# Gated unit of the S5 branch as a job inside the recurrence's stage, and the modulation's gate row by products in four column groups

## The chip, the cores and the metric

One Trainium2 chip; the kernel runs on one of its cores. The metric is the device time of one execution in microseconds (us), median over runs.

## What is computed

One layer of a hybrid block over 1024 tokens (x, 1024 by 2048) with 256 context tokens: a modulation from a condition vector, a normalised and modulated input h, a wide projection h @ w_in (2048 by 6400), three branches (an S5 state space branch, a pooling branch, a two-directional RWKV recurrence), each times a SiLU gate, an output projection, and a last layer norm.

```
shift, scale, gate = split(silu(c) @ w_ada + b_ada, 3)
h = layernorm(x) * (1 + scale) + shift
s5_u, s5_g, pool_u, pool_g, rkv, rwkv_g, w_codes, a_codes = split(h @ w_in)

y_s5 = gelu(d_skip * u + state readout)              # 1024 x 512
y_s5 = y_s5 * sigmoid(y_s5 @ w_glu + b_glu)          # the gated unit, w_glu 512 x 512
y_pool, y_rwkv = ...
out = concat(y * silu(g)) @ w_out
x_new = layernorm(ALPHA * x + gate * out) * ln_g + ln_b
```

Two pieces matter here: the gated unit (the line with w_glu), and `gate`, the last third of the modulation, a row of 2048 numbers that w_out is multiplied with. All is computed in float32; the large products split each operand into a high and a low part and add three products.

## The kernel before, in words

The program has two large stages, written by two planners that fix each engine's order when the program is built.

**The projection's stage** (`phase_ab`, `adaln`, `in_proj`). All operations there are recorded by a helper, so they carry line L300 and are told apart by their tiles. TensorE multiplies one block of 128 features of w_in after another (`pm`, three products of 128x512 for each piece: `hi,whi`, `lo,whi`, `hi,wlo`); ScalarE makes `whi` and VectorE `wlo` for each piece, up to `AHEAD` = 3 pieces ahead. Beside it run side jobs, which a planner (`Sched`) puts between the products when their inputs should be ready by its own clock: the S5 blocks (`s5_run`, 16 blocks of two groups, on two lines that follow each other), then `s5_glu`; and, on another line (`others`), `ada_gate` followed by `pool_branch`. `misc`, a pair of PSUM banks, is shared by all of them. An S5 block ends with a GELU into tile `s5y`, which one DMA of ScalarE's queue stores to DRAM (`z_ys`).

- `ada_gate` computes the gate row. Each of 64 pieces of w_ada (`agraw`, 128x512) is multiplied by its 128 numbers of silu(c) and added to an accumulator on VectorE (`agacc`); after 16 pieces one product with a column of ones (`agone`) adds up the partitions. The row is stored as `z_mgate`.
- `s5_glu` is last on the S5 line. It loads w_glu and, in 32 DMAs, all of S5's output (`gluy`), and then, for each of four blocks of 128 features, makes 8 products of 128x512 in float32 (k = 0 to 3, two halves of the tokens), a sigmoid (`glus`), and on VectorE the products with the S5 output and with the SiLU gate (`glug`); a DMA stores the result in `z_y`.

**The recurrence's stage** (`phase_c`). Key tiles (`kq`, 512 KB each, 80 segments in all) are loaded by SyncE into a ring of `KEPT` = 13 tiles. For each segment TensorE makes a Gram matrix (`gp`), which VectorE masks (`aq`). Eight segments form a batch; a batch goes through DRAM (`flat`) into a triangular solve on VectorE (`solve`, lines L1880 and L1882: 62 operations in sequence, `tmp` and `nn`), and back. A `prefix` per pair of heads (`ping`) and then the recurrence itself follow: 8 pairs, each 16 steps that TensorE, ScalarE and VectorE pass on to each other (`banky`, `banku`, lines L2023 to L2067). In the gaps a planner (`Pace`) puts other jobs by rank, lowest first: jobs of the segments (0), `prefixes` (0.5), `solver` (1), finishing work (1.5), segment loads and Gram matrices (2), and the early part of the output projection (`out_first`, ranks 2.5 to 5: `ofacc`, the first 12 of 16 blocks of w_out's rows). Within an engine's queue, SyncE's too, the order so written is fixed: an instruction that waits holds up everything behind it.

The last part (`phase_d`) does the remaining output projection and the final norm.

## Time and profile before

| | |
|---|---|
| median of 3 runs | 2965.87 us (2957.72 to 2967.88) |
| the profiled execution's own time | 2957.1 us |
| its span, first to last instruction | 2955.3 us |
| TensorE busy | 2653.7 us (90%) |
| VectorE busy | 1985.1 us (67%) |
| ScalarE, GpSimd busy | 1032.9 us, 1149.9 us |
| mean granted TensorE clock | 0.947 of full speed |

The profile is one execution with every instruction's start and duration. Busy time is a sum over stages that have different limits, so what an engine's share means is read stage by stage. The profiled execution lies 8.8 us under the median of the runs.

### The profile page before, as it was taken

To read this page: it belongs to the slowest core of one execution; us is meant where nothing else is said; L and a number is where in the kernel's file an instruction comes from. 1 tells how busy PE (TensorE), PEld (TensorE's weight loads), DVE (VectorE), ACT (ScalarE), POOL (GpSimd) and SP (SyncE) were. 2 spreads that over 40 slices of the span, in tenths; PEclk is the share of its full clock that TensorE was granted. 3 is DMA by queue.
4 is the path that set the end of the run, shared out by engine and by line. 5 is a ranking of instruction groups with operands and counts; after the bars stand their busy time and mean duration, and the time that the engine had idled before them with its cause. 6 is when DMAs were issued, how large, how long until landed. Compare 5 with 4: busy or idle time off the path is not lost. (4 is left out here: it accounts for less than half of the span.)

```text
span 2955.3 us, 56419 instructions
## 1 busy us (share of the span) xinstructions
PE 2653.7 (90%) x20080; PEld 2156.8 (73%) x20080; DVE 1985.1 (67%) x4247; ACT 1032.9 (35%) x2611; POOL 1149.9 (39%) x1681
## 2 busy tenths in 40 slices
PE   7989999999999999999899777988888899789775
PEld 2258878888888887778778366877777778678664
DVE  5548235566666567888889375677876886686568
ACT  1321224444444443222222132444443444333222
POOL 0104003343333334223552033555655556456515
PEclk9999999999999999999999877999999999798898
DMA  8734646666666665656443466665665666646744
GB/s 282 259 114 139 153 120 176 159 168 191 180 172 170 171 182 144 169 158 169 117 122 110 148 225 158 182 181 154 185 187 161 177 165 178 157 126 188 239 152 159
DMA packets 698674, 498.49 MB, mean 169 GB/s; under 512 B 347182, under 2 KB 624406, under 8 KB 695574
## 3 DMA queue, kind: packets, MB, share of 16 engines
q1 hardware_dynamic: 672632, 449.52, 54.5%
q0 software_dynamic: 6912, 24.12, 2.9%
q10 hardware_dynamic: 18848, 21.24, 2.0%
q8 instruction: 159, 2.61, 0.4%
q14 instruction: 123, 1.01, 0.1%
HBM read 339.64 MB, written 155.07 MB: 167 GB/s over the span
## 5 line engine op out<-in xcount | busy, mean ns | idle before, releaser
L300 PE MATMUL pm<-hi,whi 128*128 128x512 f32 x1600 | 511.4, 401 | 4.2 <-ACT whi L300 4.2
L300 PE MATMUL pm<-hi,wlo 128*128 128x512 f32 x1600 | 509.4, 400 | 4.3 <-DVE wlo L300 4.2
L300 PE MATMUL pm<-lo,whi 128*128 128x512 f32 x1600 | 509.2, 400 | 0.0
L300 DVE TENSOR_TENSOR wlo<-wraw,whi 128x256 fp32r<-128x256 f32 x400 | 229.2, 579 | 318.8 <-ACT whi L300 308.9
L300 PEld LDWEIGHTS pm<-hi,whi 128*128 128x128 f32 x1600 | 275.0, 190 | 58.0 <-ACT whi L300 5.8
L300 PEld LDWEIGHTS pm<-hi,wlo 128*128 128x128 f32 x1600 | 275.2, 190 | 56.1 <-DVE wlo L300 6.3
L300 PEld LDWEIGHTS pm<-lo,whi 128*128 128x128 f32 x1600 | 274.3, 189 | 51.2 <-issue 2.2
L300 ACT ACTIVATE whi<-wraw 128x256 fp32r<-128x256 f32 x400 | 160.7, 414 | 413.4 <-DMA wraw<-in_w_in 241.4
L2441 PE MATMUL ofacc<-ofhi,ofyh 128*128 128x256 f32 x768 | 250.1, 326 | 22.6 <-DVE ofev L2458 10.8
L2443 PE MATMUL ofacc<-oflo,ofyh 128*128 128x256 f32 x768 | 224.8, 293 | 3.0 <-POOL oflo L240 3.0
L2442 PE MATMUL ofacc<-ofhi,ofyl 128*128 128x256 f32 x768 | 225.1, 293 | 2.4 <-POOL ofyl L240 2.4
L1745 PE MATMUL gp<-spread,kq 128*128 128x128 f32 x1152 | 177.2, 303 | 30.5 <-ACT spread L234 12.8
L240 POOL TENSOR_TENSOR oflo<-ofw,ofhi 128x256 fp32r<-128x256 f32 x147 | 111.9, 761 | 203.2 <-ACT ofhi L234 78.0
L1745 PEld LDWEIGHTS gp<-spread,kq 128*128 128x128 f32 x1152 | 153.8, 209 | 41.5 <-DVE spread L236 12.5
L2441 PEld LDWEIGHTS ofacc<-ofhi,ofyh 128*128 128x128 f32 x768 | 153.5, 200 | 39.5 <-DVE ofev L2458 12.7
L2000 POOL TENSOR_TENSOR faded<-ping,els 64x128 f32<-64x128 f32 x304 | 127.2, 419 | 138.4 <-DVE ping L2005 125.9
L1880 DVE TENSOR_TENSOR tmp<-af,nn 128x31 f32<-128x31 f32 (+15 forms) x310 | 147.4, 476 | 22.4 <-DMA af<-flat 13.4
L1882 DVE TENSOR_TENSOR nn<-nn,tmp 128x31 f32<-128x31 f32 (+15 forms) x310 | 153.8, 496 | 10.9 <-DMA uvc<-z_v 0.2
L2442 PEld LDWEIGHTS ofacc<-ofhi,ofyl 128*128 128x128 f32 x768 | 154.7, 201 | 3.2 <-POOL ofyl L240 2.9
L2443 PEld LDWEIGHTS ofacc<-oflo,ofyh 128*128 128x128 f32 x768 | 154.4, 201 | 3.5 <-POOL oflo L240 3.5
L240 POOL TENSOR_TENSOR ofw<-ofw,ofg 128x256 f32<-128x256 f32 x143 | 115.1, 807 | 43.2 <-DMA ofw<-in_w_out 42.1
L2023 PE MATMUL banky<-ping,qt 128*128 128x128 f32 x512 | 86.9, 294 | 48.2 <-DVE ping L2005 46.4
(513 smaller groups left out, 5510.9 us busy)
## 6 DMA issues: line engine op xcount, KB each, us to landing
wraw<-in_w_in SPq DMA_DIRECT2D x400, 128.0 KB, 2.8
kq<-z_kq SPq DMA_DIRECT2D x80, 512.0 KB, 6.4
araw<-in_w_ada SPq DMA_DIRECT2D x128, 256.0 KB, 3.6
ofw<-in_w_out SPq DMA_DIRECT2D x192, 128.0 KB, 3.6
part<-ofev SPq DMA_DIRECT2D x96, 256.0 KB, 2.5
cds<-z_cd POOLq DMA_DIRECT2D x40, 512.0 KB, 5.1
z_kq<-kq SPq DMA_DIRECT2D x80, 256.0 KB, 3.1
z_kq<-kq SPq DMA_DIRECT2D x160, 128.0 KB, 3.2
```

The costliest lines, as they stand in the source:

```text
L240: (nc.vector if eng == "dve" else nc.gpsimd).tensor_tensor(out, a, b, op=op)
L300: r = x(*args, **kw)
L1745: nc.tensor.matmul(gp[:, i], seg.kb[:, i, :], qb[:, i].rearrange("p h t -> p (h t)"), start=True, stop=True)
L1880: nc.vector.tensor_tensor(tv, af[:, q, q + 1:].unsqueeze(2).to_broadcast([128, nt_, nj]), nn[:, q:q + 1, 0:nj].to_broadcast([128, nt_, nj] ...
L1882: nc.vector.tensor_tensor(nn[:, q + 1:, 0:nj], nn[:, q + 1:, 0:nj], tv, op=OP.subtract)
L2000: nc.gpsimd.tensor_tensor(to[hs], s[hs, :, hs], el[hs].to_broadcast([64, 2, 64]), op=OP.mult)
L2023: nc.tensor.matmul(b_y[:, ch.y + d], seg.qt[:, ch.c[d]], ch.s[:, d], start=(d == 0), stop=False, skip_group_check=True)
L2441: nc.tensor.matmul(o, yh[:, sl], whi, start=(first and b == 0), stop=False, skip_group_check=True)
L2442: nc.tensor.matmul(o, yl[:, sl], whi, start=False, stop=False, skip_group_check=True)
L2443: nc.tensor.matmul(o, yh[:, sl], wlo, start=False, stop=last, skip_group_check=True)
```

## The change

The gated unit leaves the projection's stage. It becomes two generators (`gated_unit(0)` and `gated_unit(1)`) in the recurrence's planner, at rank `GLU_AT` = 0.4. Their memory is `GLUS` = 5 of the 13 key tiles, which they take first: four halves of S5's output fill two tiles, w_glu's columns one, gate and sigmoid two more. Work goes by halves of the tokens (`hf`) and by feature blocks (m = 0 and 2 in one generator, 1 and 3 in the other), 8 units in all: a load of w_glu's 128 columns and of the gate, four products of 128x512, a sigmoid, two products on VectorE, a store. Until all 8 are done, key segments from the ninth on are not loaded. The output projection's loads of the S5 rows wait for `fin.glu`. S5's output is stored in another layout (512 channels by 8 by 128), for which each S5 block now issues eight DMAs from ScalarE's queue in place of one. b_glu is loaded with the first vectors of the recurrence's stage (`rvec_r`, three loads in place of two).

The gate row's 64 pieces no longer pass through VectorE. silu(c) is widened to 32 columns of which only the first is not zero (`agsil`), and four products of 32x512 write their results into four groups of 32 partitions of one PSUM bank, c = 0 to 3, with one piece of w_ada each (`agraw`, now loaded two pieces per DMA). VectorE copies or adds the bank to `agacc` once for every four pieces; the product with `agone` stays.

```diff
@@ -29,6 +29,8 @@
 QUOTA = 0.8
 SLACK = 0.05
 KEPT = 13
+GLUS = 5
+GLU_AT = 0.4
 JIT = 4
 CTX_AT = 3
 SUMS = 0.8
@@ -436,7 +438,7 @@
         g.kx = scratch("z_kx", (RW, 3, NT))
         g.v = scratch("z_v", (NT, RW))
         g.u = [scratch("z_u", (32, 128, 160)), scratch("z_ub", (32, 128, 160))]
-        g.ys = scratch("z_ys", (32, 128, 128))
+        g.ys = scratch("z_ys", (512, 8, 128))
         g.s5rot = dram.tile([128, 64, 52], FT, name="s5rot")
         g.s5pw = dram.tile([128, 64, 33], FT, name="s5pw")
         g.s5c = dram.tile([128, 64, 32], FT, name="s5c")
@@ -1121,8 +1123,6 @@
 
         def s5():
             yield from s5_run(tc, A, g, sched, misc, acc)
-            yield
-            yield from s5_glu(tc, A, g, misc)
 
         def others():
             yield from ada_gate(tc, A, g, misc)
@@ -1153,29 +1153,41 @@
 
 def ada_gate(tc, A, g, ps_tile):
 
+
     nc = tc.nc
     with tc.tile_pool(name="agp", bufs=1) as p:
         ones = p.tile([128, 1], FT, name="agone")
         nc.vector.memset(ones, 1.0)
+        sil = p.tile([128, 16, 32], FT, name="agsil")
+        nc.gpsimd.memset(sil, 0.0)
+        nc.vector.tensor_copy(sil[:, :, 0:1], g.sil[:, :, 0:1])
         brow = p.tile([1, D], FT, name="agb")
         nc.sync.dma_start(brow, A["b_ada"][0:1, 2 * D:3 * D])
-        todo = [(n, k) for n in range(4) for k in range(16)]
+        todo = [(n, k) for n in range(4) for k in range(0, 16, 2)]
         raws = []
+        yield sil, ones
         for i, (n, k) in enumerate(todo):
             while len(raws) < min(3, len(todo) - i):
                 m, j = todo[i + len(raws)]
-                raw = p.tile([128, 512], FT, name="agraw", tag="agraw", bufs=3)
-                nc.sync.dma_start(raw, A["w_ada"][0, j * 128:(j + 1) * 128, 2 * D + m * 512:2 * D + (m + 1) * 512])
+                raw = p.tile([128, 2, 512], FT, name="agraw", tag="agraw", bufs=3)
+                nc.sync.dma_start(raw, A["w_ada"][0, j * 128:(j + 2) * 128, 2 * D + m * 512:2 * D + (m + 1) * 512]
+                                  .rearrange("(k p) n -> p k n", p=128))
                 raws.append(raw)
+            if k % 4 == 0:
+                yield raws[0], raws[1], ps_tile.one
+                ps = ps_tile()
             raw = raws.pop(0)
-            yield raw,
-            sc = g.sil[:, k, 0:1]
-            if k == 0:
+            for x in range(2):
+                c = k % 4 + x
+                nc.tensor.matmul(ps[32 * c:32 * c + 32], sil[:, k + x], raw[:, x], start=True, stop=True)
+            if k % 4 == 0:
+                continue
+            if k == 2:
                 ac = p.tile([128, 512], FT, name="agacc", tag="agacc", bufs=1)
-                nc.vector.tensor_scalar(ac, raw, sc, None, op0=OP.mult)
+                nc.vector.tensor_copy(ac, ps)
             else:
-                nc.vector.scalar_tensor_tensor(ac, raw, sc, ac, op0=OP.mult, op1=OP.add)
-            if k == 15:
+                nc.vector.tensor_tensor(ac, ac, ps, op=OP.add)
+            if k == 14:
                 yield ac, ps_tile.one
                 ps = ps_tile()
                 nc.tensor.matmul(ps[0:1], ones, ac, start=True, stop=True)
@@ -1641,44 +1653,8 @@
     yt = tl("s5y", [128, GB, 128])
     nc.scalar.activation(yt.rearrange("p g n -> p (g n)"), po[:, 0:128 * GB], AF.Gelu_apprx_tanh)
     ps_tile.drop(po)
-    nc.scalar.dma_start(g.ys[gs].rearrange("g p c -> p g c"), yt)
-
-
...
-def s5_glu_(tc, A, g, pool, ps_tile):
-
-    nc = tc.nc
-    w = pool.tile([128, 4, 512], FT, name="wglu")
-    nc.sync.dma_start(w, A["w_glu"][0].rearrange("(k p) n -> p k n", p=128))
...
+    for j in range(8):
+        nc.scalar.dma_start(g.ys[16 * g0:16 * (g0 + GB), j].rearrange("(g i) c -> i g c", i=16), yt[16 * j:16 * j + 16])
 
 
 class Seg:
@@ -1693,7 +1669,7 @@
         mtiles = [ps.tile([128, 512], FT, name=f"misc{j}") for j in range(2)]
         P = Pace()
         fin = Seg()
-        fin.y, fin.part, fin.hold = {}, {}, lambda: done.load >= HOLD
+        fin.y, fin.part, fin.glu, fin.hold = {}, {}, {}, lambda: done.load >= HOLD
         out_first(tc, A, g, last, P, fin)
         st = keys.enter_context(tc.tile_pool(name="cst", bufs=RING, side="right"))
         cc = ctx.enter_context(tc.tile_pool(name="cc", bufs=1))
...
@@ -1759,14 +1735,72 @@
             r0, c0 = high[h].start + 32 * bi, 64 * h + 32 * bi
             return aq.rearrange("p s c n -> p (s c) n")[r0:r0 + 32, :, c0:c0 + 32]
 
+        def keys_tile():
+            return st.tile([128, 2, 4, 128], FT, name="kq", tag="kq", bufs=KEPT)
+
+        glu = Seg()
+        glu.tiles = [keys_tile().rearrange("p a c n -> p a (c n)") for _ in range(GLUS)]
+        glu.t = 0.0
+
+        glu.y = [glu.tiles[1 + k // 2][:, k % 2] for k in range(4)]
+        glu.begun = glu.ended = 0
+
+        def glu_load(hf, t):
+            for k in range(4):
+                nc.sync.dma_start(glu.y[k].rearrange("p (j c) -> p j c", c=64),
+                                  g.ys[128 * k:128 * k + 128, :, 64 * hf:64 * hf + 64])
+                glu.t_y = P.dma(t, us=3.0)
+            glu.begun = hf + 1
+
+        def gated_unit(i):
+
+
+            w = glu.tiles[0][:, i].rearrange("p (k n) -> p k n", k=4)
+            gt, sg = (glu.tiles[3 + i][:, j] for j in range(2))
+            t_p = t_g = 0.0
+            for hf in range(2):
+                if i == 0:
+                    yield need("sp", 2.0, glu.t, ok=lambda: glu.ended == 4 * hf and done.load >= min(2, KEPT - GLUS))
+                    glu_load(hf, glu.t)
+                for m in (i, i + 2):
+                    yield need("sp", 1.0, t_p, t_g, ok=lambda: glu.begun == hf + 1)
+                    nc.sync.dma_start(w, A["w_glu"][0, :, 128 * m:128 * m + 128].rearrange("(k p) n -> p k n", p=128))
+                    t_w = P.dma(t_p, us=2.9)
+                    nc.sync.dma_start(gt, g.gate[128 * m:128 * m + 128, 512 * hf:512 * hf + 512])
+                    t_g = P.dma(t_g, us=2.9)
+                    yield need("pe", 0.95, t_w, glu.t_y, slot=misc)
+                    j, p, t = misc.take()
+                    for k in range(4):
+                        if k:
+                            yield need("pe", 0.95)
+                        nc.tensor.matmul(p, w[:, k], glu.y[k], start=(k == 0), stop=(k == 3))
+                        t_p = t = P.run("pe", 0.95, t, t_w, glu.t_y)
+                    yield need("act", 0.7, t)
+                    nc.scalar.activation(sg, p, AF.Sigmoid, bias=vec[:, o_bg + m:o_bg + m + 1])
+                    t = P.run("act", 0.7, t)
+                    misc.give(j, t)
+                    yield need("dve", 1.7, t, t_g)
+                    nc.vector.tensor_tensor(sg, sg, glu.y[m], op=OP.mult)
+                    by_token = gt.rearrange("p (c j) -> p c j", j=8)
+                    nc.vector.tensor_tensor(by_token, by_token, sg.rearrange("p (j c) -> p c j", j=8), op=OP.mult)
+                    t = P.run("dve", 1.7, t, t_g)
+                    yield need("sp", 0.6, t)
+                    nc.sync.dma_start(g.y[128 * m:128 * m + 128, 512 * hf:512 * hf + 512], gt)
+                    t_g = P.dma(t, us=2.9)
+                    glu.t = max(glu.t, t_g)
+                    glu.ended += 1
+                    if glu.ended % 4 == 0:
+                        fin.glu[hf] = glu.t
+
         def seg_job(k):
 
             seg = allsegs[k]
-            yield need("sp", 0.6, ok=lambda: done.load == k and ring.used - ring.freed < RING and k - ring.gone < KEPT)
+            yield need("sp", 0.6, ok=lambda: done.load == k and ring.used - ring.freed < RING and k - ring.gone < KEPT
+                       and (k < KEPT - GLUS or glu.ended == 8))
             ring.used += 1
-            kq = st.tile([128, 2, 4, 128], FT, name="kq", tag="kq", bufs=KEPT)
+            kq = keys_tile()
             nc.sync.dma_start(kq.rearrange("p a c n -> p (a c n)"), g.kq[seg.src].rearrange("p a c n -> p (a c n)"))
-            t_b = seg.t_kb = P.dma(ring.out[k - KEPT] if k >= KEPT else 0.0, us=3.2)
+            t_b = seg.t_kb = P.dma(ring.out[k - KEPT] if k >= KEPT else glu.t, us=3.2)
             seg.kb, seg.qr, seg.el = kq[:, 0], kq[:, 1], els[:, seg.src]
             done.load += 1
             seg.made = True
@@ -2312,6 +2346,8 @@
         for n in range(2):
             P.add(SOLVE, solver(n))
         P.add(0.5, prefixes())
+        for n in range(2):
+            P.add(GLU_AT, gated_unit(n))
         for k in range(8):
             P.add(2, seg_jobs(k))
         P.add(1.5, finishes(pairs[:-1]))
@@ -2386,6 +2422,9 @@
                 if row >= 8:
                     yield need("any", 0.0, ok=lambda: all((row - 8, 2 * hf + q) in fin.y for q in range(2)))
                     t_raw = max(t_raw, max(fin.y[row - 8, 2 * hf + q] for q in range(2)))
+                if row < 4:
+                    yield need("any", 0.0, ok=lambda: hf in fin.glu)
+                    t_raw = max(t_raw, fin.glu[hf])
                 yield need("sp", 0.6, t_raw)
                 nc.sync.dma_start(raw, g.y[row * 128:(row + 1) * 128, hf * 512:(hf + 1) * 512])
                 t = P.dma(t_raw, us=2.9)
```

How this moves instructions is seen in each engine's order. On TensorE, at the end of the projection (`pm` are its last products, `plu,wpl` the pooling branch's, `gluy,wglu` the gated unit's, `ident,kq` and `gp` the recurrence stage's first), before:

```order
L300 MATMUL pm<-hi_1182,whi 128x512 x2
L300 MATMUL pm<-lo_1183,whi 128x512 x2
L300 MATMUL pm<-hi_1182,wlo 128x512 x2
L300 MATMUL misc<-plu,wpl 128x512 x2
L300 MATMUL misc<-gluy,wglu 128x512 x32
L489 MATMUL misc_15794<-ident,rvec_r 128x16
L1827 MATMUL misc_15794<-ident,kq 128x128 x4
```

and now, at the same place (`misc<-kq 128x512` are the gated unit's products, from key tiles):

```order
L302 MATMUL pm<-hi_1182,whi 128x512 x2
L302 MATMUL pm<-lo_1183,whi 128x512 x2
L302 MATMUL pm<-hi_1182,wlo 128x512 x2
L491 MATMUL misc_15760<-ident,rvec_r 128x20
L1861 MATMUL misc_15760<-ident,kq 128x128 x4
L1721 MATMUL gp_15832<-spread_15828,kq 128x128 x4
L1861 MATMUL misc_15761<-ident,kq 128x128 x4
L1776 MATMUL misc_15760<-kq 128x512 x3
L1721 MATMUL gp_15833<-spread_15828,kq 128x128 x4
L1776 MATMUL misc_15760<-kq 128x512
```

The 32 products that stood in one row between the stages are strewn over the start of the recurrence's stage. All 32 stand ahead of the first step of the recurrence, and the early output projection (`ofhi,ofyh` and its two companions) has 92 rows of each kind there in place of 104. The pooling branch's last products now stand 226 projection products (of 4800) before the end, S5's last block 168 before it (40 before).

On VectorE, in the first triangular solve of the recurrence's stage (`tmp` and `nn` are the solve; `kq<-kq` are the two products of a gated unit, L1783 and L1785), now:

```order
L1783 TENSOR_TENSOR kq<-kq 128x512
L1785 TENSOR_TENSOR kq<-kq 128x512
L1914 TENSOR_TENSOR tmp<-af,nn 128x31
L1916 TENSOR_TENSOR nn<-nn,tmp 128x31
...
L1914 TENSOR_TENSOR tmp<-af,nn 128x156
L1916 TENSOR_TENSOR nn<-nn,tmp 128x26x6
L1783 TENSOR_TENSOR kq<-kq 128x512
L1785 TENSOR_TENSOR kq<-kq 128x512
```

Before, nothing but four additions of the output projection stood inside that solve. Now the fifth unit stands just ahead of it and the sixth, seventh and eighth after its 12th, 28th and 40th operation; the first four stand among the masks before it. The four `ping` operations of the first prefix, which stood at the end of the second solve and behind it (after its 56th and 62nd operation), now stand after its 4th, 8th, 20th and 40th.

On SyncE's queue, now, around the last two stores of the gated unit (`z_y<-kq`; the ninth and following key loads are L1802, `flat<-nn` the first store after the first solve):

```order
L1788 DMA z_y<-kq 128x512
L2391 DMA ofw<-in_w_out 128x256
L2502 DMA part<-ofev 128x2x256
L2502 DMA part<-ofev 128x2x256
L1788 DMA z_y<-kq 128x512
L1802 DMA kq<-z_kq 128x1024 x2
L2502 DMA part<-ofev 128x2x256
L1802 DMA kq<-z_kq 128x1024 x6
L1925 DMA flat<-nn 64x1024
```

Before, the ninth key load stood four loads of the output projection behind the eighth; now eight key loads follow the last gated unit's store and stand just ahead of the end of the first solve.

## Rows read from the trace of the kernel before

**Rows 1.** Stages: length, busy PE, PEld, DVE, ACT, POOL (instructions), clock, DMA, GB/s

```profile
1190.00:1405.00 215.00, 206.29 (x986) 168.60 (x985) 183.11 (x285) 56.06 (x98) 60.70 (x55) 0.98 0.59 165
1405.00:1642.80 237.80, 222.52 (x1067) 183.82 (x1065) 206.91 (x263) 56.02 (x98) 105.57 (x77) 0.97 0.43 119
1642.80:1690.30 47.50, 34.35 (x68) 13.71 (x68) 12.30 (x10) 7.70 (x10) 1.55 (x4) 0.86 0.41 124
1690.30:1832.60 142.30, 100.23 (x954) 92.63 (x954) 95.85 (x205) 38.77 (x87) 52.26 (x70) 0.77 0.70 206
1832.60:2768.00 935.40, 818.05 (x10778) 716.01 (x10778) 673.56 (x1665) 378.18 (x1059) 525.95 (x958) 0.93 0.63 171
```

**Rows 2.** Timeline, end of projection to first key load: start, us, instructions, [idle before]

```profile
1642.17 0.63 PE L300 MATMUL pm<-hi,wlo 128*128 128x512 f32 x2
1642.83 1.02 ACT L300 ACTIVATE e<-pm 128x1024 f32<-128x1024 f32 x1 [8.40 <-PE pm L300]
...
1659.41 27.14 PE L300 MATMUL misc<-gluy,wglu 128*128 128x512 f32 x58 [1.68 <-DMA gluy<-z_ys]
...
1689.11 0.31 SPq L484 DMA_DIRECT2D rvec_r<-in_gn_w  x1
...
1690.27 6.35 SPq L1768 DMA_DIRECT2D kq<-z_kq  x8
```

**Rows 3.** Timeline, solves of batches one and two, first recurrence step

```profile
1739.05 0.18 DVE L1880 TENSOR_TENSOR tmp<-af,nn 128x31 f32<-128x31 f32 x1
...
1771.61 0.19 DVE L1882 TENSOR_TENSOR nn<-nn,tmp 128x31 f32<-128x31 f32 x1
...
1785.43 0.19 DVE L1880 TENSOR_TENSOR tmp<-af,nn 128x31 f32<-128x31 f32 x1 [1.51 <-DMA af<-flat]
...
1816.10 0.19 DVE L1882 TENSOR_TENSOR nn<-nn,tmp 128x31 f32<-128x31 f32 x1
...
1832.58 0.71 PE L2023 MATMUL banky<-ping,qt 128*128 128x128 f32 x4 [0.18 <-DVE ping L2005]
```

**Rows 4.** Waits of TensorE, 1190 to 1405 (first row), 1405 to 1643 (second)

```profile
PE misc L300 <- DVE s5rm L300: 6.9, 3, 2.8
...
PE misc L300 <- DVE s5kh L300: 10.4, 2, 8.0
```

**Rows 5.** The gate row's operations on VectorE: ns min/median/max, first and last start

```profile
L300 DVE SCALAR_TENSOR_TENSOR agacc<-agraw,sil,agacc x60: 723/746/2052, 1193.0 to 1398.9; 128x512 f32<-128x512 f32 x60
...
L300 DVE TENSOR_TENSOR agb<-misc,agb x4: 672/675/679, 1248.0 to 1401.8; 1x512 f32<-1x512 f32 x4
```

**Rows 6.** Timeline of TensorE, one recurrence step; `128*64` is rows by columns used

```profile
1904.51 0.28 PE L2442 MATMUL ofacc<-ofhi,ofyl 128*128 128x256 f32 x1
1904.63 0.28 PE L2443 MATMUL ofacc<-oflo,ofyh 128*128 128x256 f32 x1
1904.84 0.45 PE L2053 MATMUL banku<-uv,kbn 128*64 128x64 f32 x8
1905.12 0.40 PE L2059 MATMUL banky<-uv,ar 128*64 128x64 f32 x8
...
1911.29 1.16 PE L1745 MATMUL gp<-spread,kq 128*128 128x128 f32 x8
1912.29 0.61 PE L2023 MATMUL banky<-ping,qt 128*128 128x128 f32 x4
```

**Rows 7.** S5's stores on ScalarE's queue: issue time, first and last start

```profile
L300 ACTq DMA_DIRECT2D z_ys<-s5y x16: 367/381/431, 1164.7 to 1632.2; - x16
```

**Rows 8.** Timeline of ScalarE, one copy of a weight piece

```profile
1611.88 0.42 ACT L300 ACTIVATE whi<-wraw 128x256 fp32r<-128x256 f32 x1 [2.30 <-PE pm L300]
```

**Rows 9.** The gated unit's products on VectorE: ns min/median/max, first and last start

```profile
L300 DVE TENSOR_TENSOR glus<-glus,gluy x4: 1226/1226/1226, 1666.7 to 1687.7; 128x1024 f32<-128x1024 f32 x4
L300 DVE TENSOR_TENSOR glug<-glug,glus x4: 1896/1938/1954, 1668.0 to 1692.1; 128x1024 f32<-128x1024 f32 x4
```

**Rows 10.** DMA issues, 1690.3 to 1832.6: KB each, median us to landing

```profile
kq<-z_kq SPq DMA_DIRECT2D x19, 512.0 KB, 7.2
```

32 lines of the change are left out of this document (2 added, 30 removed).

## Prediction

> **What bounds the kernel now.** First the busy times by stage [rows 1]. Up to 1642.8 us TensorE is the bound: it is busy 206.3 of 215.0 us and 222.5 of 237.8 us in the two last stretches of the projection, at a granted clock of 0.98 and 0.97, so 2.4 GHz nearly all the time. VectorE is not far behind, 183.1 of 215.0 (85%) and 206.9 of 237.8 (87%). Between 1642.8 and 1690.3 no engine is the bound. TensorE shows 34.4 of 47.5 us there, but that is one job's products waiting in turn for loads, the sigmoid and VectorE (12.3 us busy). In the start of the recurrence's stage (1690.3 to 1832.6) every engine has room: TensorE 100.2 of 142.3 us at a clock of 0.77, VectorE 95.9, DMA 0.70. From 1832.6 to 2768.0 TensorE is busy 818.1 of 935.4 us.
>
> Second the timeline at the border [rows 2]. The last projection product starts at 1642.17 and takes 0.63, so it ends at 1642.80; the first key load is issued at 1690.27. The reader is to see that these 47.5 us belong to the gated unit alone: 58 of its 64 matmul instructions run from 1659.41 on, and the recurrence's first loads stand behind its last gate load in SyncE's queue.
>
> Third the timeline of the start [rows 3]: first solve from 1739.05 to 1771.80, second from 1785.43, first step of the recurrence at 1832.58. Counted from the first key load: 48.8 us to the first solve, 32.8 in it, 13.6 between the solves, 47.2 from there to the first step. This is a chain of latencies with VectorE's two solves in it, not a full engine.
>
> **The change, part by part.** Durations are those of the profiled execution (2957.1 us, span 2955.3, 8.8 us under the median of the runs).
>
> *The border.* The gated unit's 47.5 us go. What stays between the last product and the first key load are the short loads: 1690.27 - 1689.11 = 1.16 us before, with one more of 0.31 now 1.5 us [rows 2]. The last gate row's evacuation (1642.83, 1.02 us) may hold memory that the first loads need; I add 1.0. So 2.5 in place of 47.5: **-45**. Bounds: -46, and -40 if the store of that row holds them too.
>
> *The gate row, on TensorE.* 64 products, 16 sets of four, each set 8 matmul instructions of 512 columns, since a float32 product is two instructions (the gated unit shows 64 for 32 products). The trace has no products in four column groups, so the price has ends. One instruction of 512 columns takes 27.14/58 = 0.468 us [rows 2], a set one after another 3.74. Two groups are seen [rows 6]: `kbn`, four products on 64 columns each, two groups in turn, starts 8 instructions in 1905.12 - 1904.84 = 0.28 us. `gp`, 8 instructions with twice the moving columns on the whole array, takes 1912.29 - 1911.29 = 1.00, so half of that, 0.50, would be one after another. Two groups therefore run abreast, in 0.56 of the time. Going to the narrower shape costs 0.21 - 0.12 = 0.09 (start of `kbn` after L2443, against L2443 after L2442), 0.18 both ways. A set is then 0.94 + 0.18 = 1.12 us four abreast, 2.09 + 0.18 = 2.27 if only two run abreast, 3.92 one after another; 16 sets 17.9, 36.3 or 62.7 us. I take 17.9, because the row shows as many abreast as there are groups. It counts in full, TensorE being the bound there.
>
> The Trainium skill (TensorE: Matmul & The Clock Gate, Part 3) gives 2.38 times for three column groups of 512 columns, not three; carried to four groups, an estimate, this is 3.17 times, a set of 1.36 us, and the sum would be 4 us higher. The same part says that matmuls start strictly in order, which is rival two below; no row here shows four groups.
>
> *The gate row, on VectorE.* Removed: 64 operations, 60 of them at 0.746 us, 47 us in all; added: 16 reads of a bank, nearest row `agb` with 512 elements, 0.675 each, 10.8 [rows 5]. VectorE loses 36 us between 1190 and 1400. TensorE gains only what it waited: it idles 24.0 us in the two stretches, and its two largest waits for VectorE are 6.9 and 10.4 us [rows 1, 4]. The first lies where the relief is; the second where the pooling branch's long operations stay. I take 8 back. Bounds: 20 back, or none and 10 more lost, because the S5 blocks are now packed more densely (six of them within 324 projection products). Projection together: 18 - 8 = **+10** (-2 to +28 four abreast).
>
> *S5's stores.* 112 more issues on ScalarE's queue at 0.381 = 43 us, in bursts of 8, 3.0 us [rows 7]. ScalarE is busy 25% there [rows 1]. Its copies `whi`, queued behind such a burst, run ahead as far as their buffers allow: it sits 2.30 us waiting for TensorE to give one up [rows 8]. Three pieces ahead are 36 matmuls at 206.29/986 = 0.21 us, 7.5 us, more than twice the burst: price 0. Without that cover 16 x 3.0 = 49 us could show.
>
> *The gated unit in the start.* It brings 64 x 0.468 = 30 us to TensorE, which idles 42 us there; 4 x (1.226 + 1.938) = 12.7 us to VectorE, which idles 46 [rows 1, 9]; ScalarE, with 8 sigmoids more, is busy 38.8 us there. It also brings 8 MB of transfers: at 206/0.70 = 294 GB/s that is 27 us, where 0.30 x 142.3 = 43 us are free [rows 1]. So it fits in amount; what it costs is latency on the chain:
> - Half of its transfers, 13.6 us, now go among the first eight key tiles, whose loads already take 7.2 us to land [rows 10]. Half of that delays the first solve: +7.
> - The fifth unit stands just ahead of the solve and three within it, 4 x 1.58 = 6.3, and 2 for waits of VectorE for them, with the solve queued behind: +8.
> - The ninth key tile now comes only behind the last store. Eight loads, 4 MB, 14 us, are issued shortly before the first solve ends; the 13.6 us to the second solve become about 20: +6.
> - The first prefix, whose last operation came 16 us after the second solve (1816.3 to 1832.58), now stands within that solve, and the first step can start about when the solve ends: -16.
>
> Together **+5**. Ends: -16, if the units hide wholly; +35, if their transfers (27) and VectorE work (12.7) all go on the chain, less a part of the prefix's gain.
>
> *Behind the start.* 92 in place of 104 rows of each of the three `ofacc` products stand ahead of the first step, so 36 come later at 0.12 us [rows 6]: **+4**, TensorE being busy 87% there. The reads of the S5 rows need the unit's result only in the third part of the early projection, 256 `ofhi,ofyh` rows in, far behind the unit: 0.
>
> Sum: -45 + 10 + 5 + 4 = **-26**, so 2957.1 - 26 = 2931 on the profiled execution's scale. The runs' median lies 8.8 above it; I add half: **2936 us**.
>
> **The rivals.**
>
> One, the forecast.
>
> Two, column groups only two abreast. A set's second pass in a group can't start before its first; if TensorE starts instructions strictly in order, only the second pass of one product overlaps the first of the next. For it: the trace has no more than two groups at work. Against: in `kbn` both groups run abreast at full gain. 36.3 in place of 17.9: +18, 2954 us.
>
> Three, the other side: the four products of a set run one after another, because they stream four different operands. Place: 16 sets in the projection's stage, where TensorE is the bound. Price: 62.7 in place of 17.9, +45, 2981 us, slower. It decides from 1.12 + 30/16 = 3.0 us a set. Against it: `kbn` and `ar`, whose groups also stream different operands.
>
> Four, the start is already full. SyncE's queue is fixed: a store of the unit that waits for VectorE holds the key loads and w_out's behind it, and VectorE waits inside the solve for a unit whose loads are late. For it: 7.2 us to landing in that stretch, and each unit passes through four transfers in turn. Against it: 30% of DMA free, and the prefix moved forward. Start +35 in place of +5: 2966 us, no change.
>
> Five, more is freed: 20 us of TensorE's waits instead of 8, and the start loses nothing (-13 in place of +5): -30, 2906 us. For it: VectorE at 85% was what S5 waited for, and TensorE's clock in the start, 0.77 with gaps, may rise with more products in them.
>
> **How the numbers follow.** Chances: one 0.50 (own range 2918 to 2956), two 0.12, three 0.09, four 0.13, five 0.16. A measurement of this kernel tells about 0.3%, 9 us, from no change; the limits are then 2957 and 2975. Faster: nearly all of one and five, half of two, a little of four: 0.73. Same: the rest of two, most of four, some of three: 0.18. Slower: 0.09. The range from 2904 to 2970 leaves out a part of five below (0.07) and, above, most of three and some of four (0.13).
>
> **What would show it.** In the changed profile the first key load stands 2 to 5 us behind the last projection product, and that product ends near 1653. Sets of `agraw,agsil` start 8 instructions within about 1 us (two: 2.1, three: 3.7). The first solve starts 50 to 60 us after the first key load and takes about 40; the first step of the recurrence follows the key load by 140 to 155 us (four: over 170). From there to the end it is 1123 us as before, some 4 more. The prediction is wrong if the sets are slow, if the last S5 block or a held store moves the border behind the last product, or if VectorE stands idle in the first solve waiting for a unit's gate.

## Result and the profile after

The changed kernel takes 2976.87 us (median of 7 runs, 2970.51 to 2985.85); the kernel before, run beside it, 2957.76 (7 runs, 2953.11 to 2967.88). The ratio is 1.006, 95% interval 1.0042 to 1.0079: 0.6% slower, where the prediction had it 0.73 likely to be faster. The profiled execution took 2976.53 us, its span is 2974.7. Both kernels were later profiled a second time (spans 2960.9 and 2974.8), so each stage can be told apart from chance. In us, first and second profile:

| stretch | before | after | change (means) | predicted |
|---|---|---|---|---|
| projection: end of its last product | 1642.8, 1645.8 | 1664.8, 1668.1 | +22 | +10 |
| border: to the first key load | 47.5, 47.5 | 5.1, 5.1 | -42 | -45 |
| start: first key load to first step | 142.3, 139.9 | 167.4, 168.0 | +27 | +5 |
| recurrence: first to last `banky` product | 935.3, 939.2 | 943.0, 937.1 | +3 | +4 |
| behind the recurrence, to the end | 187.4, 188.5 | 194.4, 196.4 | +7 | (in the +4) |

The stages of the changed kernel, in the view of [rows 1] (length, busy PE, PEld, DVE, ACT, POOL, clock, DMA share, GB/s):

```profile
1190.00:1405.00 215.00, 202.94 (x1021) 147.93 (x1020) 161.85 (x245) 47.36 (x82) 77.67 (x70) 0.98 0.57 163
1405.00:1664.80 259.80, 248.95 (x1179) 205.12 (x1177) 182.66 (x255) 62.19 (x112) 82.48 (x63) 0.99 0.37 102
1664.80:1669.90 5.10, 0.20 (x1) 0.13 (x1) 0.18 (x1) 1.02 (x1) 0.56 (x2) 1.00 0.43 143
1669.90:1837.30 167.40, 124.35 (x921) 98.39 (x921) 99.19 (x186) 42.96 (x92) 57.08 (x71) 0.80 0.71 207
1837.30:2780.00 942.70, 830.07 (x10818) 726.68 (x10818) 672.18 (x1686) 378.09 (x1053) 528.46 (x955) 0.92 0.64 170
```

VectorE has room now in the projection (161.9 of 215.0 us; 183.1 before), and the projection is longer all the same. The start is longer, although no engine is much fuller in it (TensorE 74% busy, 70% before; DMA 0.71, 0.70). So the loss is in waits. A set of the gate row's products, and the border, in the timeline (start, us, instruction, count):

```profile
1190.44 1.06 PE L302 MATMUL misc<-agraw,agsil 128*32 128x512 f32 x8
1191.43 0.73 PE L302 MATMUL pm<-hi,whi 128*128 128x512 f32 x2
```

```profile
1664.82 1.02 ACT L302 ACTIVATE e<-pm 128x1024 f32<-128x1024 f32 x1 [10.91 <-PE pm L302]
...
1665.87 0.35 ACTq L302 DMA_DIRECT2D z_gate<-e  x1
...
1669.88 0.83 SPq L1802 DMA_DIRECT2D kq<-z_kq  x2
```

The set holds TensorE for 0.99 us (1190.44 to 1191.43): four abreast, as forecast (1.12). The border lies between the forecast and the bound that it gave for a held store: the first key load waits for the store of the last gate row (`z_gate`), 3.5 us on SyncE's queue, not for its evacuation alone.

What is new in the projection is on ScalarE. Its waits from 1184 us to the last product, before and after (waiting engine, line, for whom: us in total, times, longest):

```profile
ACT whi L300 <- DMA wraw<-in_w_in: 124.8, 34, 9.3
...
ACT whi L300 <- PE pm L300: 63.0, 32, 4.4
...
DVE wlo L300 <- ACT whi L300: 48.2, 26, 5.9
```

```profile
ACT whi L302 <- DMA wraw<-in_w_in: 105.7, 44, 6.7
...
DVE wlo L302 <- ACT whi L302: 90.6, 25, 9.7
ACT whi L302 <- DMA z_ys<-s5y: 73.2, 13, 8.0
...
ACT whi L302 <- PE pm L302: 25.9, 14, 3.6
```

And one burst of S5's stores:

```profile
1360.48 7.89 ACTq L302 DMA_DIRECT2D z_ys<-s5y  x8
...
1368.42 1.03 ACT L302 ACTIVATE whi<-wraw 128x256 fp32r<-128x256 f32 x3 [7.97 <-DMA z_ys<-s5y]
...
1368.89 0.73 PE L302 MATMUL pm<-hi,whi 128*128 128x512 f32 x2 [0.92 <-ACT whi L302]
```

The largest wait of a copy `whi` is for the loads of w_in, before and now. The next was for TensorE to give a buffer back (63.0 us): there the copies ran ahead. Now it is behind a burst of stores (73.2 us), and the wait for TensorE is down to 25.9. This burst took 7.9 us, not the 3.0 of eight times one issue [rows 7], and the cover of three pieces (7.5 us in the prediction) was used up: TensorE waited 0.92 us for the copy.

The start, in the view of [rows 3]:

```profile
1736.56 0.19 DVE L1914 TENSOR_TENSOR tmp<-af,nn 128x31 f32<-128x31 f32 x1 [3.12 <-DMA af<-flat]
...
1775.67 0.19 DVE L1916 TENSOR_TENSOR nn<-nn,tmp 128x31 f32<-128x31 f32 x1
...
1811.42 0.19 DVE L1914 TENSOR_TENSOR tmp<-af,nn 128x31 f32<-128x31 f32 x1 [8.09 <-DMA af<-flat]
...
1837.26 1.01 PE L2057 MATMUL banky<-ping,qt 128*128 128x128 f32 x3 [2.82 <-DVE ping L2039]
```

Counted from the first key load: 66.7 us to the first solve (48.8 before), 39.3 in it (32.8), and from its end to the first step 61.4 (60.8). The second solve starts 35.6 us behind the first one's end (13.6 before) and the first prefix is moved forward, as the order said; at the first step the two cancel.

### The profile page after: what moved, and what is told of

Read it like the earlier page. It is cut to its first block, busy times and chain, and to the rows that moved or that the text cites. A ratio compares the mean times of both kernels' runs of the same rounds, so it can differ in the third digit from the quotient of the medians.

```text
span 2974.7 us, 56582 instructions
## 1 busy us (share of the span) xinstructions
PE 2683.0 (90%) x20207; PEld 2166.8 (73%) x20207; DVE 1936.9 (65%) x4196; ACT 1028.0 (35%) x2601; POOL 1163.1 (39%) x1689
## 4 chain that ended last, share of the span: by engine, by line
PE 59%; DVE 17%; DMA 11%; issue 4%; SPq 4%; POOL 2%; ACT 2%; ACTq 0%; POOLq 0%; DVEq 0%
PE pm L302 30%; PE misc L302 5%; PE pc L302 4%; PE gp L1721 4%; DVE tmp L1914 3%; PE ada L302 3%; DVE nn L1916 3%; PE ofacc L2480 2%; SPq L302 2%; DMA kq<-z_kq 1%; PE ofacc L2481 1%; PE ofacc L2482 1%; PE banky L2057 1%; DVE ping L2039 1%; DMA wraw<-in_w_in 1%
## 5 line engine op out<-in xcount | busy, mean ns | idle before, releaser
L302 PEld LDWEIGHTS pm<-hi,whi 128*128 128x128 f32 x1600 | 273.2, 189 | 66.3 <-ACT whi L302 12.2
```

The costliest lines, as they stand in the source:

```text
L302: r = x(*args, **kw)
```

## The experiments

The theory after the result had four parts: S5's eight stores on ScalarE's queue cost the projection 7 to 8 us; the unit's work costs the start; the gain from the moved prefix is none; and the order of the early output projection behind the start is worth more than the +4 given to it. The rivals were a too dense packing of the S5 blocks by the planner (it takes a set for 3.41 us where the chip takes 0.99), a start that only waits for the ninth key tile, and chance in the recurrence. Of each run the stretches are read as in the table above.

**The two halves of the change, each alone.** `ada_alone` is the kernel before with the new `ada_gate` and nothing else; `glu_alone` is the changed kernel with the old `ada_gate`.

> The gate row by products in column groups alone; the gated unit, S5's store and everything behind the projection stand as before. Theory 'stores' (the 16 sets cost 17 us and 8 us of TensorE's waits for S5 come back; what else was lost in the changed kernel's projection came from S5's eight stores a block on ScalarE's queue): the last projection product ends about 9 us later than before, near 1652, and the runs are 1.003 of before. Rival 'packing' (the planner takes a set for 3.4 us, packs the S5 blocks too densely and TensorE waits for them): all of the changed kernel's loss is here, the last product ends near 1664 and the runs are 1.007 of before.

> The gated unit's move alone (with S5's eight stores a block), the gate row on VectorE as before. Theory 'stores': projection +7 to +10, border -42, start +25, behind it +15: 5 to 8 us slower than before, 1.002. Rival 'packing': projection +0, so 2 us faster than before or equal. If the recurrence's later +15 belongs to the gate row's products and not to the unit, 10 us faster, 0.997.

Measured: `ada_alone` 2967.15 us, 1.0024 of before (1.001 to 1.0038); `glu_alone` 2996.38, 1.0121 (1.0093 to 1.0149). They don't add: +7 and +36 us alone, +19 together. Neither theory had this, and the stages say much of why (columns as in the stages above: `ada_alone`, then `glu_alone`):

```profile
1405.00:1686.70 281.70, 271.55 (x1210) 212.19 (x1208) 171.64 (x229) 71.96 (x121) 68.06 (x53) 1.00 0.40 117
1686.70:1691.70 5.00, 0.26 (x2) 0.13 (x1) 0.17 (x1) 1.02 (x1) 0.56 (x2) 0.72 0.40 146
```

```profile
1405.00:1628.20 223.20, 212.00 (x990) 173.32 (x990) 170.70 (x225) 51.63 (x91) 93.64 (x71) 0.96 0.37 102
1628.20:1693.80 65.60, 22.51 (x77) 16.09 (x75) 54.62 (x59) 4.06 (x6) 19.13 (x17) 0.58 0.26 70
```

With the gate row on TensorE and one store a block, S5 is done early: its last store is issued at 1553.2 us (1632.2 before, 1630.3 in the changed kernel). The gated unit, still in its old place, then runs between the projection's products, and the border is 5.0 us without any move of the unit. But its 64 instructions (28.8 us busy in this profile) and the 16 sets now stand in a stretch in which TensorE is the bound, so the first key load comes when it came before (1691.7; 1690.3 and 1693.2 in the two profiles of before). Up to the first step nothing is lost; in this profile the 7 us of the medians lie in the recurrence (945.2 us), whose instructions are those of before, and why is not shown. With VectorE's gate row and eight stores a block, S5's last store is issued at 1686.0: the projection ends early, at 1628.2, and 65.6 us of S5's last three blocks and the pooling branch stand behind it, VectorE busy 54.6 of them. The border moved; it did not go. So the unit's move needs the gate row's products, with which S5 ends early enough. The eight stores make S5 end later again (next run).

**One store a block.** All of a block's bytes in one issue; the rows lie in another order in memory, so the unit works on permuted rows.

```
-    for j in range(8):
-        nc.scalar.dma_start(g.ys[16 * g0:16 * (g0 + GB), j].rearrange("(g i) c -> i g c", i=16), yt[16 * j:16 * j + 16])
+    nc.scalar.dma_start(g.ys[16 * g0:16 * (g0 + GB)].rearrange("(g i) j c -> (i j) g c", i=16), yt)
```

> The changed kernel with one store of an S5 block in place of eight (the same bytes; the rows lie in another order in memory, so the unit works on permuted rows). Theory 'stores': the ScalarE queue is held 0.4 us in place of 3.7 to 8 at the end of each of the 16 blocks, the copies whi are no longer late, and the last projection product ends 7 us earlier than in the changed kernel, near 1658; runs 0.9975 of it. Rival 'packing': under 2 us of difference.

Measured: 2967.76 us; the last product ends at 1656.9, 7.9 us earlier than in the changed kernel, and S5's last store is issued at 1556.2. The waits of `one_perm` in the same stretch:

```profile
ACT whi L302 <- DMA wraw<-in_w_in: 82.0, 26, 8.7
ACT whi L302 <- PE pm L302: 72.4, 30, 5.6
...
DVE wlo L302 <- ACT whi L302: 54.4, 19, 6.9
```

`whi` runs ahead again, and the gain has the expected size: the stores cost it. A too dense packing is out, since here the S5 blocks are packed denser and the projection is shorter. But the expectation took the rest to stand as in the changed kernel, and it does not. The planner counts every DMA's issue on its own clock (0.45 us in `Clock`), and with eight of them it places the blocks later: behind S5's last product stand 168 projection products in the changed kernel, 438 here (438 in `ada_alone` too, 40 before). TensorE runs them in that order, so the 74 us by which S5's last store is earlier (1556.2 against 1630.3) are written in the order; they don't show S5 waiting for its own stores. TensorE's own waits for `whi` and `wlo`, from 1119 us to the last product, are 7.8 us in the changed kernel and 4.9 here. So some 3 of the 7.9 us are late copies; how much of the rest is the order and how much the bursts, no run tells apart.

**The stores on SyncE,** one step of the block behind the gelu, each row where the changed kernel has it:

```
+    yield 2
     for j in range(8):
-        nc.scalar.dma_start(...)
+        nc.sync.dma_start(...)
```

> The changed kernel with S5's eight stores a block issued by SyncE, one step of the block behind the gelu, in place of ScalarE; the rows lie where the changed kernel has them. Theory 'stores on ScalarE hold S5 and the whi copies': S5's last store is issued near 1556 as with one store a block (changed kernel 1630), the last projection product ends near 1656 to 1658, and the time is 8 us under the changed kernel's, 0.9975 of it, near 2968. Rival 'the queue only moves': a store that waits for the gelu holds the loads of w_in behind it on SyncE, TensorE waits for them, and the time is the changed kernel's or more.

Measured: 2962.74 us, 1.0013 of before (1.0003 to 1.0024), 14 us under the changed kernel's median. The last product ends at 1657.7, as expected; S5's last store stands at 1597.9, later than expected but ahead of the border. This order differs too: 272 projection products stand behind S5's last product. The rival (loads of `w_in` held) shows in `whi`, which waits 152.6 us for them (105.7 in the changed kernel), yet hardly in TensorE, whose waits for `whi` and `wlo` are 7.0 us from 1119 us on (7.8). Of the 14 us, 7 stand in the projection of this profile. The rest of this profile's gain is in the recurrence (929.4 us), which varies by as much; why the medians too differ by more than the projection is not shown. The projection itself varies: it ends between 1654.6 and 1664.1 in the six kernels below and here that have the stores on SyncE (mean 1658.1), and between 1664.8 and 1668.8 in the five profiles with the changed kernel's projection (1667.0), so the gain is about 9 us.

**The unit left out,** with the start and what follows otherwise as changed:

> The changed kernel without the gated unit's jobs: its loads, products, sigmoids, multiplications and stores are left out, key tiles nine to thirteen wait for nothing, and the early output projection reads the gate's rows in place of the unit's result. Theory 'unit on the chain' (the unit costs 41 us in the start: forecast 21, and the prefix's 16 are a real gain): the first step follows the first key load by about 126 us in place of 167, and the time is about 41 to 50 us under the changed kernel's, 2927 to 2935. Rival 'the start does not gain from the prefix': 142 us as before, about 2950. Rival 'the clock': if the 15 us behind the first step stay, they are not the unit's.

Measured: 2940.02 us (0.9933 of before, 0.9906 to 0.9959), 37 us under the changed kernel, where the two theories gave 41 to 50 and about 27. The first step follows the first key load by 134.1 us: the unit costs the start 33 us. The 126 of the first theory took the prefix's 16 us for a gain of its own; without the unit the prefix stands behind the second solve again, since it had only been moved because that solve was late. Behind the first step its profile has 1126.6 us, where the changed kernel has 1137.4 and 1133.5 and before 1122.7 and 1127.7, so most of the loss there goes with the unit as well. The start is 6 to 8 us under before's, 4.5 of them ahead of the first solve; why was not tested.

**Eight key tiles first.** The unit's first loads behind eight key loads in place of two:

```
-                    yield need("sp", 2.0, glu.t, ok=lambda: glu.ended == 4 * hf and done.load >= min(2, KEPT - GLUS))
+                    yield need("sp", 2.0, glu.t, ok=lambda: glu.ended == 4 * hf and done.load >= min(8, KEPT - GLUS))
```

> The changed kernel with the gated unit's first loads behind eight key loads instead of two. Theory 'ninth key': the second solve hangs on the ninth key tile (44 us from its load to the solve, as 49 us from the first load to the first solve before), which hangs on the end of the unit; so the first solve comes 8 us earlier behind the first key load (58 in place of 67), but the unit ends as late as before, the gap between the solves grows by as much, and the first step stays 165 to 168 us behind the first key load. Rival 'first keys': the 9 us that keys three to eight wait for the unit's loads are what the start loses; then the step comes at 158 and the time falls by 9.

Measured: 2947.31 us, 0.996 of before (0.9945 to 0.9975), the first complete kernel here that beats it. But the start did not change: 168.0 us, and the first solve not 58 but 68 us behind the first key load. The 30 us come from a place that neither theory named. Products `ofacc` of the early output projection ahead of and behind the recurrence's last product (stretch, length, busy TensorE and instructions of `ofacc` alone, clock, DMA): before, changed, eight keys first.

```profile
1832.60:2768.00 935.40, 282.84 (x1830) 0.93 0.63 171
2768.00:2955.30 187.30, 22.47 (x162) 0.84 0.53 178
```

```profile
1837.30:2780.40 943.10, 288.03 (x1818) 0.92 0.64 170
2780.40:2974.70 194.30, 30.40 (x210) 0.82 0.54 179
```

```profile
1840.60:2779.90 939.30, 301.12 (x1926) 0.93 0.65 175
2779.90:2944.60 164.70, 12.57 (x90) 0.83 0.55 187
```

The recurrence takes the same time with 108 products more in it (939.3 and 943.1 us), and the stretch behind it is 29.6 us shorter. TensorE's whole busy time in that stretch is 15.5 us less (113.8 against 129.3); the other 14 us are waits, which were not taken apart. The planner writes its order from what is ready when; another place for the unit's first loads gave another order for a thousand microseconds. In the changed kernel 210 products are left behind the recurrence, 48 more than before, and that stretch is 7 us longer.

**Again, without an edit,** both kernels:

> The kernel before, a second time, for a second profile. If the time behind the first step (1122.7 us in its first profile, 1133.3 with the gate row alone, whose instructions there are the same) varies by itself, it lies between 1122 and 1136 here; the start and the border stay within 2 us of 142.3 and 47.9.

> The changed kernel, a second time, for a second profile: the last projection product within 2 us of 1664.8, the start within 2 us of 167.4, the time behind the first step between 1127 and 1140 (first profile 1137.4).

Measured: before, 939.2 us in the recurrence and 188.5 behind it (together 1127.7; first profile 1122.7); changed 937.1 and 196.4 (1133.5; 1137.4). `ada_alone`, whose instructions from the border on are those of before, has 945.0 and 188.3. So the recurrence varies by 10 us with one order, and the stretch behind it by 2: the first can't be read for a few us, the second can. The starts of before (142.3, 139.9, and 139.9 in `ada_alone`) and of the changed kernel (167.4, 168.0) hold their difference. Two figures differ by more than the 2 us that were expected: before's start (2.4 less), and the end of the changed kernel's projection (1668.1, 3.3 more).

**Both mends together,** the stores on SyncE and eight keys first:

> Both mends together: S5's stores on SyncE, and the gated unit's first loads behind eight key loads. In the order of this kernel 90 products of the early output projection (ofacc) stand behind the recurrence's last product, as with the key loads first alone; in the changed kernel 210, in the one before 162. Theory 'stores and order add': projection 7 us shorter and the stage behind the recurrence 30 us shorter than in the changed kernel, so 2935 to 2942 and 0.993 of before. Rival 'the two share a gain': not under 2947, the time with the key loads first alone.

Measured: 2942.72 us, 0.9938 of before (0.9916 to 0.996): 0.6% faster than before, 1.2% under the changed kernel. The profile has the last product's end at 1656.3, a start of 168.1 and 163.8 us behind the recurrence. In the stages the stores' gain and the order's add. In the medians that is not clear of noise: 4.6 us under `keys_first` alone, and the two intervals overlap (0.9916 to 0.996, 0.9945 to 0.9975).

**The unit ranked behind the recurrence's jobs** (`GLU_AT = 1.7`), on top of both mends:

> As both mends together, with the gated unit ranked behind the recurrence's own jobs (GLU_AT 1.7 in place of 0.4). By the order the first solve is not interrupted, six of the eight units stand before the first step, the second solve only behind the first steps, and no product of the early output projection stands behind the recurrence's last one. Theory 'order': the first step comes 140 to 150 us behind the first key load in place of 168, the stage behind the recurrence ends 165 us or less after it, but the second solve, which waits for the unit's end and 44 us more, holds the recurrence between. Net 2925 to 2950. Rival 'TensorE-bound recurrence': every product moved ahead of the recurrence's end costs its time there, and the time is that of both mends together.

Measured: 2969.78 us, 1.0036 of before (1.0022 to 1.005). The start is 160.1, where 140 to 150 was expected: the first solve still starts 69.4 us behind the first key load, with four units ahead of it. No `ofacc` product is left behind the recurrence (155.0 us), as expected, but the second solve starts 192 us behind the first key load (142 in the changed kernel, 95 before), and the recurrence takes 983.7, 44 more than with both mends. That the second solve would hold it was expected, not by how much; the forecast of the sum was too low.

**Half of the unit,** 512 of the 1024 tokens, in the changed kernel:

> The changed kernel with the first half of the gated unit alone (512 of 1024 tokens; the second half's loads, products, sigmoids, multiplications and stores are left out, and the output projection reads the gate there). Theory 'ninth key': the ninth key tile is loaded about 48 us behind the first key load in place of 97, the second solve no longer waits for it and follows the first within about 15 us in place of 36, and the first step comes 140 to 150 us behind the first key load in place of 167. Rival 'the unit's own work': the start falls by half of the unit's 33 us, to about 151, with the gap between the solves still over 25 us.

Measured: 2952.9 us in one run, and both fall. The ninth key tile is loaded 46.7 us behind the first and the second solve follows the first by 13 us, as expected; the first step still comes 165.8 us behind the first key load. Its first solve starts 67 us behind that load and ends at 1778.3, and the step comes 61.4 us later, as in the changed kernel, whose second solve is late, and as before, whose prefix is. So the step follows the first solve, and that is late with half of the unit as with all of it. The first `ping` of the prefix shows how the second solve takes part. It adds the result of a product (`misc<-uvc,kbnc`); first the kernel before, then the changed one:

```profile
1808.50 0.45 PE L2124 MATMUL misc<-uvc,kbnc 128*64 128x64 f32 x8
...
1812.51 0.59 DVE L2005 TENSOR_TENSOR ping<-faded,misc 64x128 f32<-64x128 f32 x2
```

```profile
1808.08 0.69 PE L2158 MATMUL misc<-uvc,kbnc 128*64 128x64 f32 x8
...
1812.29 0.59 DVE L2039 TENSOR_TENSOR ping<-faded,misc 64x128 f32<-64x128 f32 x2
```

The product ends 37 us behind the first solve's end before, 33 now. Then `ping` stands some 3.5 us behind the second solve in VectorE's order, in both: before behind its 56th operation, now behind its fourth, where VectorE waited for that solve's load. From `ping` to the step it is 20 us before and 25 now.

**What makes the first solve late.** Three edits on top of both mends: the second half's loads behind the stores that feed the first solve (`batches[0].ready == 2`), and the unit's first loads behind the products of eight, or of four, key tiles (`done.gram >= 8`, `>= 4`).

> Both mends, and the second half of the gated unit's loads behind the stores of the matrices that the first solve loads (flat<-aq), which stand behind those loads in SyncE's queue with both mends (last mask product 1711.9, second group of stores 1720.0). Theory 'held store': of the 20 us by which the first solve is later than without the unit (69.1 against 44.5 behind the first key load), 8 are this hold; the first solve comes 61 us behind the first key load, and the first step about 160 behind it, 61 us after the first solve ends, as in every profile so far. Rival 'products between': the hold is covered by something else and the first solve stays at 67 to 69. In this order 156 products of the early output projection are left behind the recurrence (both mends: 90), so its stage behind the recurrence takes about 185 and the whole is not faster.

> Both mends, and the unit's first loads behind the products of the first eight key tiles. Theory 'products between': the unit's products, sigmoids and multiplications stand between the first key tiles' products and masks on in-order engines and make the rest of the delay; the first solve then comes 45 to 50 us behind the first key load, as without the unit (44.5), the first step 61 us behind that solve's end, 142 to 148 in all. But the unit's end, the ninth key tile and the second solve come late (over 170 behind the first key load) and the recurrence waits for the second solve, 20 to 45 us as with the unit ranked later (44). 18 products left behind it: stage behind the recurrence 155 to 165. Net 2935 to 2960. Rival 'transfers': the first solve stays over 55 although no unit stands ahead of it.

> Both mends, and the unit's first loads behind the products of four key tiles. Between the two others: the first solve 52 to 62 us behind the first key load, the first step 61 us behind that solve's end, the ninth key tile at 100 to 110 and the second solve at 145 to 155 behind the first key load, early enough for the recurrence not to wait for it. 138 products left behind the recurrence: that stage 175 to 185. Net 2940 to 2955, no faster than both mends alone, since what the start gives the order behind it takes. Rival 'start alone decides': 2930 to 2935.

Measured: `flat_first` 2964.2 us in one run, first solve at 68.1 (68.9 with both mends), first step at 178, where 160 was expected. The stores stand at 1712.7, early, but now the solve's load `af<-flat` stands behind the unit's loads in SyncE's queue (issued at 1721.6), and it takes 6.2 us from issue to the solve, 3.8 with both mends. So taking the hold from the stores gave nothing. `grams_first` 2953.14 (0.9962 of before, 0.994 to 0.9985): first solve at 45.8, first step at 134.8 (142 to 148 was expected). `grams_half` 2961.24 (0.9981, 0.9964 to 0.9999; 2940 to 2955 was expected): first solve at 68.7, where 52 to 62 was expected, first step at 179.8, 12 us later than with both mends. In `grams_first`, with no unit ahead of those products, the 22 us are gone, while `keys_first` had shown that the keys' loads alone don't give them back. The mask of the eighth key tile tells where they go (changed, `grams_half`, `grams_first`; a solve needs all eight masks):

```profile
1720.41 0.69 DVE L1726 TENSOR_TENSOR aq<-gp,masks 128x512 f32<-128x512 f32 x1 [0.20 <-PE gp L1721]
```

```profile
1718.34 0.69 DVE L1727 TENSOR_TENSOR aq<-gp,masks 128x512 f32<-128x512 f32 x1
```

```profile
1696.18 0.68 DVE L1727 TENSOR_TENSOR aq<-gp,masks 128x512 f32<-128x512 f32 x1
```

Behind the first key load that is 50.5, 49.2 and 29.7 us; before 34.0, and 31.8 without the unit. Wherever it is late, four units stand ahead of it on TensorE, in `grams_half` too: there five of the eight masks come early, but the last one does not, so half of the way gives nothing back. It is the unit's work, loads included, between the first key tiles' products, on engines that take their instructions in the order written. TensorE of the changed kernel in that stretch:

```profile
1694.53 2.08 PE L1776 MATMUL misc<-kq 128*128 128x512 f32 x2 [3.81 <-ACT kq L1779]
1696.40 1.06 PE L1861 MATMUL misc<-ident,kq 128*128 128x128 f32 x4
1697.25 1.92 PE L1776 MATMUL misc<-kq 128*128 128x512 f32 x2
1698.96 1.89 PE L1721 MATMUL gp<-spread,kq 128*128 128x128 f32 x8
```

A unit's products (`misc<-kq`) waited for the sigmoid of another unit (3.81 us), and the key tile's products (`gp`) stood behind them. What `grams_first` wins in the start it pays in the recurrence, whose second solve comes late (stretches: start; recurrence):

```profile
1666.50:1801.30 134.80, 108.42 (x848) 80.45 (x849) 75.11 (x145) 38.25 (x82) 45.20 (x61) 0.84 0.79 232
1801.30:2803.00 1001.70, 870.57 (x11092) 761.64 (x11091) 712.11 (x1735) 389.65 (x1090) 554.40 (x994) 0.92 0.63 170
```

Its second solve starts at 1830.21, 164 us behind the first key load, 29 behind the first step, and the recurrence is 62 us longer than with both mends, where 20 to 45 was expected. "61 us in every profile" was too strong: it is 57.5 to 63.0 where the second solve starts between the first one's end and the step, 50.7 and 55.0 where it stands behind the step (`grams_first`, `unit_later`), and 66.3 and 68.3 in `grams_half` and `flat_first`; why there was not tested.

The orders that were run give nearly one line for the stretch behind the recurrence: 155.0 us with no product left (160.0 in `half_unit`, which has none either), 157.5 with 18, 163.8 and 164.7 with 90, 178.9 with 138, 188.9 with 156, 187.3 with 162, 194.3 with 210. From 90 to 210 that is 0.25 us a product. A product itself is 0.14 us busy (30.40 us for 210), so the number tells the length but is not its whole cause.

## Why the prediction was wrong

**Right.** *The border:* -42 for -45, inside the bounds given, and for the reason that they name. *The gate row on TensorE:* 16 sets at 0.99 us are 16 us, and with the waits in or behind four of them they held TensorE for 19.3; 17.9 was forecast, and rivals two and three are out. The price one after another was too high: the 0.468 us of [rows 2] mixes both levels of TensorE's clock: the granted clock was 0.5 (1.2 GHz) up to 1663.5 us and 1.0 (2.4 GHz) behind, and the starts of the unit's instructions stand 0.85 us apart at first and 0.43 later. At the full clock eight are 3.43 us, so four abreast gain 3.5 times. The Trainium skill (TensorE: Matmul & The Clock Gate, Part 3) has 2.38 times for three column groups, which carried to four, an estimate, is 3.17; the 3.5 measured here goes past it. *VectorE's relief:* the waits of TensorE for results of the S5 blocks fell from 21.9 to 13.0 us (1184 us to the last product), 9 where 8 were forecast.

**"S5's stores ... price 0".** This step failed, worth 7 to 9 us in the projection, shown by `one_perm` and `sync_store`. A burst was priced as eight times one issue, 3.0 us, and set against the lead of `whi`; the bursts took 3.6 to 7.9. That alone is little: TensorE's waits for `whi` and `wlo` are 3 us more than with one store a block. What was not thought of at all is that the planner prices the issues too and writes another order, with S5's last block 270 projection products later than with one store. In this kernel that lag stays in the projection's shadow; in `glu_alone` it becomes the border. How the 7 to 9 us divide between bursts and order is open. The Trainium skill (DMA: Bandwidth & Descriptors, Issuing engines are not separate DMA queues) says that issuing from several engines only saves the time on the sequencer, usually small beside the DMA itself. Here the 16 bursts were 84 us of ScalarE's queue, 6 with one store a block, and the median issue 0.43 us where its DMA took 2.0 to land; what of it reached TensorE is the open share.

The other 3 to 5 us of the projection's miss were not tested. The product that waits for the gate row's sum (`misc<-agacc`, 3.7 us at the one place) is a candidate.

**"+6" for the ninth key tile and "-16" for the prefix.** Together -10; measured +0.6. The first step came 60.8 us behind the first solve's end before and 61.4 after, and it comes 61.4 behind it in `half_unit` too, where the second solve is early and the prefix stands where it stood. The prefix went into the second solve because that solve was late: what it gives is what the late solve takes. The first `ping`, 3.6 us behind its product before and 3.5 now, shows that the second solve held it by as much as ever. The row stood in [rows 3], from 1771.61 to 1832.58; I cut it at the second solve, as if the step hung on that one, and took a shift for a gain. The ninth key tile's own price was also too small: from its load to the second solve it is 44 us (1767.18 to 1811.42), about what the first solve needs from the first load (48.8), not the 14 of the transfer.

**"+7" and "+8" ahead of and within the first solve.** The places were right, and within the solve the size too: +6.5 for 8. Ahead of it this step failed, +18 for 7. I priced transfers that share a bandwidth. What delays the solve is the fixed order: four units, each a chain of load, products, sigmoid, multiplications and store, stand between the eight key tiles' products, and the eighth mask comes 16.5 us later (50.5 against 34.0). "So it fits in amount" was right and of no use. Rival four had such a hold, on VectorE and SyncE, with +35, and was given 0.13.

**"Behind the start: +4".** The term counted products ahead of the first step. What counts is how many are left when the recurrence ends: 210 against 162, 7 us, and 90 in `keys_first`, 30 us the other way. The order told these counts before any run; I read it at the start alone. The rest of the 15 us between the first profiles is no more than the recurrence varies by with one order.

Sum in means: 22 - 42 + 27 + 3 + 7 = +17, against +19 in the medians.

## What to carry to other kernels

When work moves into a stage written by a planner, follow its order to the end of the kernel: what the move does to the rows that are left over a thousand microseconds later can be worth more than the move. A gap without a full engine is not free room on engines with in-order queues; look for the chain whose end the next stage waits for, and price each instruction that is put between its links. And price a burst of DMA issues by a burst's length, not by one issue, and twice: where a late copy hurts, and in the planner's clock, where it moves whatever is placed by that clock. A run that takes the burst away changes both.

## What the runs showed of the hardware

A DMA issue on ScalarE's queue is 0.31 to 0.44 us mostly, but up to 1.3 us within a burst, and eight of 16 KB each took 3.6 to 7.9 us; one issue of the same 128 KB took 0.37. Four products of 32 stationary columns in four column groups, 512 moving columns each, take 0.99 us with the shape changes on both sides, where one float32 product of 512 columns on the whole array takes 0.86 at the full clock (two instructions, 0.43 us from start to start in `ada_alone`). One program's recurrence, with the same instructions in the same order, took 935.3, 939.2 and 945.0 us in three profiles.
